# The seven products of a down projection issued between the last row tiles of the up projection, with five operands split step by step

## The chip, the core and the metric

One core of one Trainium2 chip runs the whole layer in one launch. The metric is device time in microseconds (us) of one execution; lower is better. The core has a matrix engine (TensorE, PE in the rows; PEld is its weight load), VectorE (DVE), ScalarE (ACT), GpSimd (POOL), SyncE (SP), and 16 DMA engines.

## The reference, cut to what matters

One decoder layer on 512 tokens of width 1024. The change lies in its feed-forward part:

```python
up = causal_dwconv(h @ w_up, conv_w, conv_b)      # 1024 -> 2*2816, width 3
val, gate = up[..., :D_FF], up[..., D_FF:]
ffn = (silu(gate) * val) @ w_down                 # 2816 -> 1024
h = layer_norm(ALPHA * h + ffn + ple)
```

Everything is float32. A product of two float32 matrices is formed from rounded high parts and the low parts left over (`mm3`: high x high, high x low, low x high), so each operand is first split: ScalarE copies the high part, VectorE subtracts it to give the low part.

## The kernel before, in words

**Up projection** (`ffn_up`, L1188). D_FF = 2816 makes NF = 22 row tiles f of 128 features; each has a value half (b = 0) and a gate half (b = 1). A half is 24 matmuls (8 chunks of the 1024 inputs, three each) into one PSUM bank of 128 x 512, and then a convolution: one ScalarE activation (L1200) and two VectorE multiply-adds (L1201, L1202, by the helper at L292). After both halves ScalarE does Silu (L1204, recorded at L299). A weight half tile is 512 KB; `Weights` fetches it on SP's queue (L103), splits it with a ScalarE cast (L120) and a VectorE subtraction (L121), and `use(n)` splits one ahead and fetches three ahead.

**Tiles 0 to 15** are the first 2048 rows of the down projection. They go through `combine` (L1220): even and odd tiles are paired (p = 0 to 7), tokens are cut into two halves, and the pair gives the seven left operands of a seven-product scheme for 2 x 2 block matrices (A11, S3, S2, A22, S1, A12, S4). The first four are split at once (pages `sa`, L1249 to L1252); S1, A12 and S4 are kept raw and split in one go before the product that reads them (`split_left`, L1263). **Tiles 16 to 21** are split as they come (`act`, L1208 to L1212) and multiplied in the plain way at the end.

**Right operands** (`Products`, L171). The 2048 rows of `w_down` are 2 x 2 blocks of 4 parts each. `ORDER` lists the seven right operands: three are plain blocks (products 0, 5, 6), one is a fresh block that gets a second one subtracted (product 1), and three reuse an earlier raw part and add another block (products 2, 3, 4). Subtracting is done by a ScalarE multiply by -1 (L207) and an accumulating DMA issued by GpSimd (L208), 16 of them in all. Each part is then split (L219, L220). With 7 products of 4 parts there are 28 steps, numbered 0 to 27 here; `use(n)` splits up to step n + 1 and fetches up to step n + 5.

**Down projection** (`ffn_down`, L1276). A step is 12 matmuls (2 sub-parts, 2 row blocks of 128 tokens, three each). The products accumulate in PSUM pairs X, Y and V; four of them are added to the residual in between (`add`, L1306). Then come tiles 16 to 21 with six plain weight tiles (`WD`), 162 matmuls, and the layer norm and stores (L1344 to L1361).

**What sets the order.** `run` (L1364) goes through `ffn_up` to its end and then calls `ffn_down`. The order in which each engine meets its instructions is set at build time by a planner that follows the program's order as a priority, its own model of durations, and the dependencies; each engine's queue then runs strictly in that order on the chip. Only where `self.in_order` is true (L263) are all matmuls tied to the program's order; it is false from L1390 on.

**Buffers.** `Pages` (L44) hands out 51 SBUF buffers of 128 x 1024 float32, first freed first reused. A buffer that is handed out again may be written only when the readers of its earlier content are done. So a short list of free buffers means that a fetch or a split waits for recent work. PSUM has 8 banks, handed out in the same way (`Banks`, L73).

**Fetching for the down projection** begins in the last two row tiles (L1213 to L1215): after tile 20 step 0 is split and step 1 fetched, after tile 21 step 1 is split and step 2 fetched. The layer norm's two vectors are loaded after product 2 (L1322, L1323).

Of the kernel before, what the change touches and what calls it, by code (L numbers as in the profile page):

```python
# [12 lines left out]
F32 = mybir.dt.float32  # L13
F32R = mybir.dt.float32r
I32 = mybir.dt.int32
AF = mybir.ActivationFunctionType
ALU = mybir.AluOpType

P = 128
T = 512  # L20
# [5 lines left out]
NF = DFF // P  # L26
# [3 lines left out]
NPAGES, NHALVES = 37, 6  # L30
NPAGES_LATE = 14
NS = 8
LAG_B, LAG_C = 5, 7
QK_RATIO, G_RATIO = 6.5 / 6, 7 / 6
SPLIT_AHEAD = 1
# [135 lines left out]
class Products:  # L171
# [14 lines left out]
    def __init__(self, tc, pages, blocks, fetch_ahead=5, split_ahead=1):  # L186
        self.nc, self.pages, self.blocks = tc.nc, pages, blocks
        self.fa, self.sa = fetch_ahead, split_ahead
        self.per = NS // 2
        self.raw, self.hl = {}, {}  # L190
# [45 lines left out]
class Layer:  # L236
    def __init__(self, tc, cst, pages, banks, a):
# [18 lines left out]
        self.W = Weights(tc, pages, srcs)  # L256
        self.WD = Weights(tc, pages, [a["w_down"][i] for i in range(NF - 2 * NS)], halved=False)
        self.WP = Products(tc, pages, a["w_down_blocks"])
# [927 lines left out]


    def ffn_up(self):  # L1188
        nc = self.nc
        self.act, self.left, self.now = [], {}, ([], [])  # L1190
        for f in range(NF):
            yp = self.pages.get(f"cv{f}", F32, (P, 2, T))
            for b in range(2):
                bank = self.banks.get(f"up{f}{b}")
                for _ in self.feature_mms(self.wup + 2 * f + b, bank, self.hT):
                    pass
                y = yp.t[:, b]
                cw = self.cw[:, b * NF + f]
                cb = self.cb[:, b * NF + f:b * NF + f + 1]
                nc.scalar.activation(y, bank.t, AF.Identity, scale=cw[:, 2:3], bias=cb)  # L1200
                self.stt(y[:, 1:], bank.t[:, 0:T - 1], cw[:, 1:2], y[:, 1:], ALU.mult, ALU.add)  # L1201
                self.stt(y[:, 2:], bank.t[:, 0:T - 2], cw[:, 0:1], y[:, 2:], ALU.mult, ALU.add)  # L1202
                bank.free()
            self.actf(3, yp.t[:, 1], yp.t[:, 1], AF.Silu)  # L1204
            if f < 2 * NS:
                self.combine(f, yp)
            else:
                self.tt(yp.t[:, 0], yp.t[:, 0], yp.t[:, 1], ALU.mult)  # L1208
                pg = self.pages.get(f"act{f}", F32R, (P, 2, T))
                self.split(pg.t[:, 0], pg.t[:, 1], yp.t[:, 0])  # L1210
                yp.free()
                self.act.append(pg)  # L1212
            if f >= NF - 2:  # L1213
                self.WP.split_to(f - NF + 3)
                self.WP.fetch_to(f - NF + 4)  # L1215
            yield
        for pg in self.hT:
            pg.free()

    def combine(self, f, yp):  # L1220

        nc, p = self.nc, f // 2
        first, last = slice(0, T // 2), slice(T // 2, T)
        y0, y1 = yp.t[:, 0], yp.t[:, 1]
        if f % 2 == 0:

            self.sq = self.pages.get(f"sq{p}", F32, (P, 4, T // 2))
            self.tt(self.sq.t[:, 0], y0[:, first], y1[:, first], ALU.mult)  # L1230
            self.tt(y0[:, last], y0[:, last], y1[:, last], ALU.mult)
            self.even = yp
            return
        sq, q = self.sq.t, p % 4
        if q == 0:
            for name in ("S1", "A12", "S4"):
                self.left.setdefault(name, []).append(self.pages.get(f"{name}{p}", F32, (P, 4, T // 2)))
        s1, a12, s4 = (self.left[name][-1].t[:, q] for name in ("S1", "A12", "S4"))
        a21 = self.even.t[:, 0, last]
        self.tt(a12, y0[:, first], y1[:, first], ALU.mult)  # L1240
        self.tt(sq[:, 3], y0[:, last], y1[:, last], ALU.mult)
        yp.free()
        self.tt(sq[:, 1], a21, sq[:, 0], ALU.subtract)
        self.tt(s1, a21, sq[:, 3], ALU.add)
        self.even.free()
        self.tt(sq[:, 2], s1, sq[:, 0], ALU.subtract)
        self.tt(s4, a12, sq[:, 2], ALU.subtract)
        for i in range(2):
            pg = self.pages.get(f"sa{p}{i}", F32R, (P, 2, 2, T // 2))  # L1249
            src = sq[:, 2 * i:2 * i + 2]  # L1250
            nc.scalar.copy(pg.t[:, :, 0], src)
            self.tt(pg.t[:, :, 1], src, pg.t[:, :, 0].bitcast(F32), ALU.subtract)  # L1252
            self.now[i].append(pg)
        self.sq.free()

    def load_conv(self):
        self.cw = self.cst.tile([P, 2 * NF, 3], F32, name="cw")
# [2 lines left out]
        self.nc.sync.dma_start(self.cb, self.a["conv_b"])  # L1260


    def split_left(self, name):  # L1263

        out = []
        for raw in self.left.pop(name):
            for i in range(2):
                pg = self.pages.get(f"sl{name}{i}", F32R, (P, 2, 2, T // 2))
                src = raw.t[:, 2 * i:2 * i + 2]
                self.nc.scalar.copy(pg.t[:, :, 0], src)  # L1270
                self.tt(pg.t[:, :, 1], src, pg.t[:, :, 0].bitcast(F32), ALU.subtract)
                out.append(pg)
            raw.free()
        return out

    def ffn_down(self):  # L1276


        nc, WP, WD, res = self.nc, self.WP, self.WD, [pg.t for pg in self.res]
        halves = (slice(0, 512), slice(512, 1024))  # L1280
        X, Y, V, Z = [], [], [], []
        ops = {}

        def now(i, o):
            return [[pg.t[:, o, x] for x in range(2)] for pg in self.now[i]]

        def left(name):
            ops[name] = self.split_left(name)
            return [[pg.t[:, o, x] for x in range(2)] for pg in ops[name] for o in range(2)]

        def product(q, bank, a, fresh, side=lambda j: None):
            if fresh:
                bank.extend(self.banks.get(f"p{q}{m}") for m in range(2))
            for j in range(WP.per):
                n = q * WP.per + j
                hi, lo = (pg.t.rearrange("p (k n) -> p k n", k=2) for pg in WP.use(n))
                for k in range(2):
                    p = 2 * j + k
                    for m in range(2):
                        ts_ = slice(m * P, m * P + P)  # L1300
                        self.mm3(bank[m].t, a[p][0][:, ts_], a[p][1][:, ts_], hi[:, k], lo[:, k],
                                 fresh and p == 0, p == NS - 1)
                WP.free(n)
                side(j)

        def add(bank, rows, col):  # L1306
            for m in range(2):
                r = res[2 * rows + m][:, halves[col]]
                self.tt(r, r, bank[m].t, ALU.add)

        def drop(pages):
            for pg in pages:
                pg.free()

        product(0, X, now(0, 0), True)
        add(X, 0, 0)
        product(1, Y, now(0, 1), True)
        drop(self.now[0])
        add(Y, 1, 1)
        product(2, X, now(1, 0), False)  # L1320
        add(X, 1, 0)
        g2 = self.bcast_load("ln2_g", "g2", nc.sync)  # L1322
        b2 = self.bcast_load("ln2_b", "b2", nc.sync)  # L1323
        a = left("S1")
        product(3, Y, now(1, 1), False)
        drop(self.now[1])
        product(4, X, a, False)
        drop(ops["S1"])
        add(X, 1, 1)
        product(5, V, left("A12"), True)  # L1330
        drop(ops["A12"])
        product(6, X, left("S4"), False, lambda j: WD.use(j))
        drop(ops["S4"])
        Z.extend(self.banks.get(f"z{m}") for m in range(2))
        KD = NF - 2 * NS
        ws = [WD.use(k) for k in range(KD)]

        q = slice(768, 1024)
# [5 lines left out]
        for t in range(4):  # L1344
            r, parts = res[t], parts_of[t]
            st, mv = self.ln_tiles(len(parts))
            ts_ = slice(t * P, t * P + P)
            for i, (c, bank, fresh) in enumerate(parts):
                for k in range(KD):
                    a, w = self.act[k].t, ws[k]  # L1350
# [13 lines left out]
    def run(self):  # L1364
# [36 lines left out]
                self.prefetch_mid()  # L1401
        for _ in self.mid():
            pass
        for _ in self.ffn_up():
            pass
        self.ffn_down()


# [43 lines left out]
def _rows(w, per):  # L1452

    k = w.shape[0] // P
    return w.reshape(k // per, per, P, w.shape[1]).transpose(0, 2, 1, 3).reshape(k // per, P, per * w.shape[1])
# [12 lines left out]
def layouts(i):  # L1468
# [18 lines left out]
        "w_up": up,  # L1487
        "w_down": _rows(i["w_down"][0][2 * NS * P:], 1),

# [35 lines left out]
```

## Time and profile before

| what | us |
|---|---|
| three runs of the kernel before | 804.79, 807.84, 809.76 |
| median | 807.84 |
| the profiled execution's own time | 807.08 |
| its span, first to last instruction | 805.3 |
| around the span (807.08 - 805.3) | 1.8 |

Times in the rows are counted from the span's start. "Busy" on PE includes modelled ends of matmuls, so the start times of matmuls are the safer reading.

### The profile page before, as it was taken

What the parts mean: (1) busy time and instruction counts of PE and PEld (TensorE: products, weight loads), DVE (VectorE), ACT (ScalarE), POOL (GpSimd) and SP (SyncE); (2) the same over time, 40 slices, a digit from 0 to 9 for tenths busy, and PEclk for the clock granted to TensorE, in tenths of its full rate; (3) what the DMA queues carried; (4) which work ended last, traced back from release to release, by engine and by line L of the source; (5) the groups of instructions that cost most, each with busy time, mean ns of one, the idle gap of its engine ahead of it and who ended that gap; (6) DMA issues with size and microseconds to landing.
All of it is one profiled execution on the core that took longest, in us unless ns stands there. A gap on an engine that the chain in (4) does not pass through costs nothing. (4 is left out here: it accounts for less than half of the span.)

```text
span 805.3 us, 9856 instructions
## 1 busy us (share of the span) xinstructions
PE 778.2 (97%) x3668; PEld 648.7 (81%) x3668; DVE 547.0 (68%) x960; ACT 366.8 (46%) x578; POOL 38.5 (5%) x81
## 2 busy tenths in 40 slices
PE   8999999999999989999999999999999998799996
PEld 7888888878888878888888888888888887578885
DVE  6866998696667958947744566666666664367656
ACT  6435667654443274514433344343434345577300
POOL 0000000000000010004300000000000002210000
PEclk9999999999999999999999999999999999899999
DMA  9913222024022584414212330224122327987202
GB/s 320 373 70 99 58 74 60 27 89 145 28 79 78 185 261 157 140 58 171 76 53 105 105 129 3 79 78 131 53 78 79 105 79 213 224 182 285 90 26 79
DMA packets 32176, 95.14 MB, mean 118 GB/s; under 512 B 4480, under 2 KB 8704, under 8 KB 31872
## 3 DMA queue, kind: packets, MB, share of 16 engines
q1 hardware_dynamic: 28240, 81.40, 29.7%
q0 software_dynamic: 3312, 12.06, 6.8%
q10 hardware_dynamic: 576, 1.05, 0.3%
q8 instruction: 29, 0.48, 0.2%
q14 instruction: 19, 0.16, 0.1%
HBM read 88.20 MB, written 3.15 MB: 113 GB/s over the span
## 5 line engine op out<-in xcount | busy, mean ns | idle before, releaser
L262 PE MATMUL up<-hT,wh 128*128 128x512 f32 x704 | 216.5, 389 | 0.0
L121 DVE TENSOR_TENSOR wl<-wr,wh 128x1024 fp32r<-128x1024 f32 (+1 forms) x113 | 135.7, 1212 | 59.5 <-ACT wh L120 43.2
L120 ACT CAST wh<-wr 128x1024 fp32r<-128x1024 f32 (+1 forms) x113 | 116.8, 1043 | 90.6 <-PE o L262 13.4
L262 PEld LDWEIGHTS up<-hT,wh 128*128 128x128 f32 x704 | 132.2, 188 | 27.3
L262 PE MATMUL up<-hT,wl 128*128 128x512 f32 x352 | 136.9, 389 | 0.0
L292 DVE SCALAR_TENSOR_TENSOR cv<-up,cw,cv 128x511 f32<-128x511 f32 x88 | 65.8, 748 | 35.6 <-ACT cv L1200 34.2
L262 PE MATMUL g<-xs,wh 128*128 128x512 f32 x256 | 81.0, 398 | 0.0
L262 PEld LDWEIGHTS up<-hT,wl 128*128 128x128 f32 x352 | 66.1, 188 | 13.7
L1200 ACT ACTIVATE cv<-up,cb,cw 128x512 f32<-128x512 f32 x44 | 34.3, 779 | 64.7 <-PE up L262 64.7
L262 PEld LDWEIGHTS g<-xs,wh 128*128 128x128 f32 x256 | 46.1, 188 | 8.6 <-issue 0.6
L220 DVE TENSOR_TENSOR dl<-dr,dh 128x1024 fp32r<-128x1024 f32 x28 | 33.7, 1222 | 24.5 <-ACT dh L219 24.5
L262 PE MATMUL g<-xs,wl 128*128 128x512 f32 x128 | 50.0, 391 | 0.0
L262 PE MATMUL p<-dh,sa 128*128 128x512 f32 x128 | 41.2, 400 | 7.3 <-ACT dh L219 7.3
L262 PE MATMUL mx<-yts,wh 128*128 128x512 f32 x128 | 39.2, 390 | 2.4 <-DVE yts L970 2.4
L262 PE MATMUL pg<-wh,hT 128*128 128x512 f32 x128 | 40.2, 390 | 0.0
L262 PE MATMUL o<-wh,mx 128*128 128x512 f32 x128 | 40.0, 391 | 0.0
L219 ACT CAST dh<-dr 128x1024 fp32r<-128x1024 f32 x28 | 28.5, 1046 | 15.6 <-DMA dr<-in_w_down_blocks_dram 15.6
L262 PEld LDWEIGHTS p<-dh,sa 128*128 128x128 f32 x128 | 24.6, 193 | 13.1 <-ACT dh L219 8.2
L262 PEld LDWEIGHTS mx<-yts,wh 128*128 128x128 f32 x128 | 23.9, 188 | 7.7 <-DVE yts L970 2.8
L208 POOL DMA_DIRECT2D dr<-in_w_down_blocks_dram x16 | 13.9, 869 | 311.4 <-ACT dr L207 311.1
L262 PEld LDWEIGHTS g<-xs,wl 128*128 128x128 f32 x128 | 24.0, 188 | 5.3
L262 PEld LDWEIGHTS pg<-wh,hT 128*128 128x128 f32 x128 | 24.0, 188 | 4.9
(213 smaller groups left out, 1390.1 us busy)
## 6 DMA issues: line engine op xcount, KB each, us to landing
wr<-in_w_up_dram SPq DMA_DIRECT2D x44, 512.0 KB, 3.3
wr<-in_w_g_dram SPq DMA_DIRECT2D x16, 512.0 KB, 3.4
dr<-in_w_down_blocks_dram SPq DMA_DIRECT2D x16, 512.0 KB, 5.2
dr<-in_w_down_blocks_dram POOLq DMA_DIRECT2D x16, 512.0 KB, 7.9
wr<-in_w_qk_dram SPq DMA_DIRECT2D x8, 512.0 KB, 9.9
wr<-in_w_glu_dram SPq DMA_DIRECT2D x8, 512.0 KB, 4.1
wr<-in_w_o_dram SPq DMA_DIRECT2D x8, 512.0 KB, 3.3
wr<-in_w_pe_gate_dram SPq DMA_DIRECT2D x8, 512.0 KB, 3.5
```

The source lines that it names most:

```text
L120: self.nc.scalar.copy(hi.t[:, c], raw.t[:, c])
L121: self.nc.vector.tensor_tensor(out=lo.t[:, c], in0=raw.t[:, c], in1=hi.t[:, c].bitcast(F32), op=ALU.subtract)
L208: self.nc.gpsimd.dma_start(pg.t, self.block(plus, j), accum_op=ALU.add)
L219: self.nc.scalar.copy(hi.t, raw.t)
L220: self.nc.vector.tensor_tensor(out=lo.t, in0=raw.t, in1=hi.t.bitcast(F32), op=ALU.subtract)
L262: ins = self.nc.tensor.matmul(out=out, lhsT=lhsT, rhs=rhs, start=start, stop=stop, skip_group_check=True).ins
L292: self.nc.vector.scalar_tensor_tensor(out=out, in0=a, scalar=s, in1=b, op0=op0, op1=op1)
L1200: nc.scalar.activation(y, bank.t, AF.Identity, scale=cw[:, 2:3], bias=cb)
```

## The change

`ffn_up` now yields twice per tile, after the value half and at the end. `run` fetches the right operands of steps 0 to 3 at tile 14, splits step 0 at tile 15, and from the value half of tile 16 on takes 1.5 steps of a generator `products()` per half tile: 18 of the 28 steps lie between halves of tiles 16 to 21, the other 10 behind them. From the first step on `in_order` is true. `combine` splits only A11 and S3 (two pairs at a time, buffer `se`); S2, A22, S1, A12 and S4 stay raw, and `products()` splits each in pieces of 128 x 512, one piece for this step and one for the next. The layer norm's vectors are loaded after step 19, and the tiles of `WD` are used from step 24, as before.

```diff
+PRODUCTS_RATIO = 1.5
...
     def ffn_up(self):
...
                 bank.free()
+                if b == 0:
+                    yield f
...
-            if f >= NF - 2:
-                self.WP.split_to(f - NF + 3)
-                self.WP.fetch_to(f - NF + 4)
-            yield
+            yield f
...
     def combine(self, f, yp):
+        if f % 4 == 0:
+            self.early = self.pages.get(f"se{p}", F32, (P, 2, 2, T // 2))
+        a11, s3 = (self.early.t[:, o, p % 2] for o in range(2))
...
-            for name in ("S1", "A12", "S4"):
+            for name in ("S2", "A22", "S1", "A12", "S4"):
...
-        for i in range(2):
-            pg = self.pages.get(f"sa{p}{i}", F32R, (P, 2, 2, T // 2))
-            src = sq[:, 2 * i:2 * i + 2]
-            nc.scalar.copy(pg.t[:, :, 0], src)
-            self.tt(pg.t[:, :, 1], src, pg.t[:, :, 0].bitcast(F32), ALU.subtract)
+        if p % 2 == 1:
+            for o, name in enumerate(("A11", "S3")):
+                self.ops.setdefault(name, []).append(self.split_pairs(name + str(p), self.early.t[:, o]))
+            self.early.free()
+
+    def split_pairs(self, name, src):
+        pg = self.pages.get(f"sl{name}", F32R, (P, 2, 2, T // 2))
+        self.nc.scalar.copy(pg.t[:, :, 0], src)
+        self.tt(pg.t[:, :, 1], src, pg.t[:, :, 0].bitcast(F32), ALU.subtract)
+        return pg
...
+    def products(self):
...
+        def operand(n):
+            if n >= len(todo) or todo[n] in split:
+                return
+            q, j = todo[n]
+            name = self.PRODUCTS[q][0]
+            if q < 2:
+                split[q, j] = ops[name][j]
+                return
+            raw = ops[name][j // 2]
+            split[q, j] = self.split_pairs(f"{name}{j}", raw.t[:, 2 * (j % 2):2 * (j % 2) + 2])
+            if j % 2 == 1:
+                raw.free()
+
+        for n, (q, j) in enumerate(todo):
...
+            hi, lo = (pg.t.rearrange("p (k n) -> p k n", k=2) for pg in WP.use(n))
+            operand(n)
+            operand(n + 1)
+            a = split.pop((q, j))
+            for k in range(2):
+                for m in range(2):
+                    ts_ = slice(m * P, m * P + P)
+                    self.mm3(self.acc[b][m].t, a.t[:, k, 0, ts_], a.t[:, k, 1, ts_], hi[:, k], lo[:, k],
+                             whole[b] == q and (j, k) == (0, 0), (j, k) == (WP.per - 1, 1))
+            a.free()
+            WP.free(n)
+            if j == WP.per - 1 and q in self.WHOLE:
...
+                    self.tt(r, r, self.acc[b][m].t, ALU.add)
+            yield q, j
...
     def run(self):
-        for _ in self.ffn_up():
-            pass
+        products, acc = None, 0.0
+        for f in self.ffn_up():
+            if f == 2 * NS - 2:
+                self.WP.fetch_to(self.WP.nf + 2)
+            if f == 2 * NS - 1:
+                self.WP.split_to(1)
+            if f >= 2 * NS:
+                if products is None:
+                    products = self.products()
+                    self.in_order, self.last_mm = True, None
+                acc += PRODUCTS_RATIO
+                while acc >= 1.0:
+                    acc -= 1.0
+                    next(products)
+        for q, j in products:
+            if (q, j) == (4, 3):
+                self.g2 = self.bcast_load("ln2_g", "g2", self.nc.sync)
+                self.b2 = self.bcast_load("ln2_b", "b2", self.nc.sync)
+            if q == 6:
+                self.WD.use(j)
         self.ffn_down()
```

## Rows read from the trace of the kernel before

**Rows 1.** The page: busy us and share of the span, by engine
```profile
PE 778.2 (97%) x3668; PEld 648.7 (81%) x3668; DVE 547.0 (68%) x960; ACT 366.8 (46%) x578; POOL 38.5 (5%) x81
```
**Rows 2.** Windows: PE, PEld, DVE, ACT, POOL busy (instructions), clock, DMA share, GB/s
```profile
680.00:690.00 10.00, 2.85 (x12) 2.12 (x11) 3.92 (x6) 7.11 (x10) 4.29 (x5) 0.81 1.06 237
690.00:700.00 10.00, 9.77 (x38) 7.42 (x37) 3.69 (x4) 6.27 (x7) 2.07 (x3) 0.85 1.06 210
...
611.40:676.70 65.30, 65.30 (x290) 54.09 (x289) 39.85 (x51) 29.49 (x37) 1.25 (x2) 1.00 0.33 103
...
731.70:764.60 32.90, 32.90 (x146) 27.22 (x146) 23.39 (x25) 19.28 (x22) 0.00 (x0) 1.00 0.44 160
```
**Rows 3.** Timeline of PE: start, us, instruction [idle before, its releaser]
```profile
676.75 0.39 PE L262 MATMUL p<-dh,sa 128*128 128x512 f32 x1
...
681.97 0.39 PE L262 MATMUL p<-dh,sa 128*128 128x512 f32 x1
689.50 1.22 PE L262 MATMUL p<-dh,sa 128*128 128x512 f32 x2 [7.15 <-ACT dh L219]
...
721.19 0.50 PE L262 MATMUL p<-dl,sa 128*128 128x512 f32 x1 [0.49 <-DVE dl L220]
...
759.63 0.61 PE L262 MATMUL p<-dh,slS 128*128 128x512 f32 x2
...
764.39 0.39 PE L262 MATMUL p<-dh,slS 128*128 128x512 f32 x1
764.61 0.39 PE L262 MATMUL p<-wh,act 128*128 128x512 f32 x1
```
**Rows 4.** Timeline of ACT in the hole
```profile
678.98 2.94 ACT L207 ACTIVATE dr<-dr 128x1024 f32<-128x1024 f32 x3
...
683.28 0.61 ACT L299 ACTIVATE cv<-cv 128x512 f32<-128x512 f32 x1
685.55 1.06 ACT L207 ACTIVATE dr<-dr 128x1024 f32<-128x1024 f32 x1 [1.66 <-DMA dr<-in_w_down_blocks_dram]
686.51 0.60 ACT L279 CAST act<-cv 128x512 fp32r<-128x512 f32 x1
687.46 1.99 ACT L219 CAST dh<-dr 128x1024 fp32r<-128x1024 f32 x2 [0.34 <-DMA dr<-in_w_down_blocks_dram]
```
**Rows 5.** Groups, 655 to 806 us: busy, mean ns | idle before
```profile
L220 DVE TENSOR_TENSOR dl<-dr,dh 128x1024 fp32r<-128x1024 f32 x28 | 33.7, 1222 | 24.5 <-ACT dh L219 24.5
L219 ACT CAST dh<-dr 128x1024 fp32r<-128x1024 f32 x28 | 28.5, 1046 | 15.6 <-DMA dr<-in_w_down_blocks_dram 15.6
L207 ACT ACTIVATE dr<-dr 128x1024 f32<-128x1024 f32 x16 | 16.6, 1054 | 6.1 <-DVE dl L220 3.9 <-DMA dr<-in_w_down_blocks_dram 2.1
...
L283 DVE TENSOR_TENSOR slS<-S,slS 128x512 fp32r<-128x512 f32 x8 | 5.3, 685 | 0.2 <-ACT slS L1270 0.2
...
L1270 ACT CAST slS<-S 128x512 fp32r<-128x512 f32 x8 | 4.7, 611 | 0.0
...
L1200 ACT ACTIVATE cv<-up,cb,cw 128x512 f32<-128x512 f32 x5 | 3.9, 779 | 3.6 <-PE up L262 3.6
```
**Rows 6.** DMA queues and issues, 676 to 712 us: share of 16 engines; KB, us to landing
```profile
q0 software_dynamic: 1584, 5.77, 81.2%
q1 hardware_dynamic: 831, 3.01, 22.6%
...
dr<-in_w_down_blocks_dram POOLq DMA_DIRECT2D x11, 512.0 KB, 8.6
dr<-in_w_down_blocks_dram SPq DMA_DIRECT2D x2, 512.0 KB, 6.9
```
**Rows 7.** Tile dr: duration ns min/median/max; landing min/median/max
```profile
L208 POOL DMA_DIRECT2D dr<-in_w_down_blocks_dram x16: 856/865/945, 665.5 to 720.8; - x16
...
DMA to landing us min/median/max: 3.1/6.4/11.2
```
**Rows 8.** Groups, 611.4 to 676.7 us (the last six row tiles)
```profile
L292 DVE SCALAR_TENSOR_TENSOR cv<-up,cw,cv 128x511 f32<-128x511 f32 (+1 forms) x24 | 18.0, 748 | 14.0 <-ACT cv L1200 13.6
```

More of the change, by code (lines that the diff above doesn't have):

```diff
@@ L1189, in ffn_up @@
         nc = self.nc
-        self.act, self.left, self.now = [], {}, ([], [])
+        self.act, self.ops = [], {}
         for f in range(NF):
@@ L1220, in combine @@
     def combine(self, f, yp):
-        nc, p = self.nc, f // 2
+        p = f // 2
         first, last = slice(0, T // 2), slice(T // 2, T)
         y0, y1 = yp.t[:, 0], yp.t[:, 1]
+        if f % 4 == 0:
+            self.early = self.pages.get(f"se{p}", F32, (P, 2, 2, T // 2))
+        a11, s3 = (self.early.t[:, o, p % 2] for o in range(2))
         if f % 2 == 0:
-            self.sq = self.pages.get(f"sq{p}", F32, (P, 4, T // 2))
-            self.tt(self.sq.t[:, 0], y0[:, first], y1[:, first], ALU.mult)
+            self.tt(a11, y0[:, first], y1[:, first], ALU.mult)
             self.tt(y0[:, last], y0[:, last], y1[:, last], ALU.mult)
@@ L1233, in combine @@
             return
-        sq, q = self.sq.t, p % 4
-        if q == 0:
-            for name in ("S1", "A12", "S4"):
-                self.left.setdefault(name, []).append(self.pages.get(f"{name}{p}", F32, (P, 4, T // 2)))
-        s1, a12, s4 = (self.left[name][-1].t[:, q] for name in ("S1", "A12", "S4"))
+        if p % 4 == 0:
+            for name in ("S2", "A22", "S1", "A12", "S4"):
+                self.ops.setdefault(name, []).append(self.pages.get(f"{name}{p}", F32, (P, 4, T // 2)))
+        s2, a22, s1, a12, s4 = (self.ops[name][-1].t[:, p % 4] for name in ("S2", "A22", "S1", "A12", "S4"))
         a21 = self.even.t[:, 0, last]
         self.tt(a12, y0[:, first], y1[:, first], ALU.mult)
-        self.tt(sq[:, 3], y0[:, last], y1[:, last], ALU.mult)
+        self.tt(a22, y0[:, last], y1[:, last], ALU.mult)
         yp.free()
-        self.tt(sq[:, 1], a21, sq[:, 0], ALU.subtract)
-        self.tt(s1, a21, sq[:, 3], ALU.add)
+        self.tt(s3, a21, a11, ALU.subtract)
+        self.tt(s1, a21, a22, ALU.add)
         self.even.free()
-        self.tt(sq[:, 2], s1, sq[:, 0], ALU.subtract)
-        self.tt(s4, a12, sq[:, 2], ALU.subtract)
-        for i in range(2):
-            pg = self.pages.get(f"sa{p}{i}", F32R, (P, 2, 2, T // 2))
-            src = sq[:, 2 * i:2 * i + 2]
-            nc.scalar.copy(pg.t[:, :, 0], src)
-            self.tt(pg.t[:, :, 1], src, pg.t[:, :, 0].bitcast(F32), ALU.subtract)
-            self.now[i].append(pg)
-        self.sq.free()
+        self.tt(s2, s1, a11, ALU.subtract)
+        self.tt(s4, a12, s2, ALU.subtract)
+        if p % 2 == 1:
[7 more added lines that the diff above has]
+        return pg
     def load_conv(self):
@@ L1260, in load_conv @@
         self.nc.sync.dma_start(self.cb, self.a["conv_b"])
[L1263 to L1274, printed above, removed]
+    PRODUCTS = (("A11", "X"), ("S3", "Y"), ("S2", "X"), ("A22", "Y"), ("S1", "X"), ("A12", "V"), ("S4", "X"))
@@ new lines @@
+    WHOLE = {0: (0, 0), 1: (1, 1), 2: (1, 0), 4: (1, 1)}
+    def products(self):
+        WP, ops = self.WP, self.ops
+        self.acc = {}
+        todo = [(q, j) for q in range(len(self.PRODUCTS)) for j in range(WP.per)]
+        split, whole = {}, {}
+        def operand(n):
[11 more added lines that the diff above has]
+        for n, (q, j) in enumerate(todo):
+            name, b = self.PRODUCTS[q]
+            fresh = b not in self.acc
+            if fresh:
+                self.acc[b] = [self.banks.get(f"{b}{m}") for m in range(2)]
+                whole[b] = q
+            hi, lo = (pg.t.rearrange("p (k n) -> p k n", k=2) for pg in WP.use(n))
[10 more added lines that the diff above has]
+            if j == WP.per - 1 and q in self.WHOLE:
+                rows, col = self.WHOLE[q]
+                for m in range(2):
+                    r = self.res[2 * rows + m].t[:, 512 * col:512 * col + 512]
+                    self.tt(r, r, self.acc[b][m].t, ALU.add)
+            yield q, j
@@ L1276, in ffn_down @@
     def ffn_down(self):
-        nc, WP, WD, res = self.nc, self.WP, self.WD, [pg.t for pg in self.res]
+        nc, WD, res = self.nc, self.WD, [pg.t for pg in self.res]
         halves = (slice(0, 512), slice(512, 1024))
[L1281 to L1334, printed above, removed]
+        X, Y, V = (self.acc[b] for b in "XYV")
+        g2, b2 = self.g2, self.b2
@@ L1335, in ffn_down @@
+        Z = [self.banks.get(f"z{m}") for m in range(2)]
         KD = NF - 2 * NS
```

## The prediction

> **What bounds the kernel now.** I read the page first: the matrix engine is busy for 97% of the span [rows 1], so only its idle time and its slow time can be won back. The windows by stage show where these lie [rows 2]. While the last six row tiles of the up projection run (611.4 to 676.7 us) PE has no idle time at clock 1.00, and so it is again from 731.7 to 764.6. Between them it is busy for 2.85 of 10 us, then for 9.77 of 10 but at a granted clock of 0.81 and 0.85. The timeline of PE gives the place [rows 3]: the first product matmul starts at 676.75, steps 0 and 1 run, and at 681.97 PE stops for 7.15 us until the high part of step 2 is there; short waits follow, one of 0.49 at 721.19.
>
> ScalarE's timeline says why [rows 4]. Its queue has three multiplies for the accumulating transfers (678.98, 2.94 us) ahead of the Silu of tile 21 (683.28), and a fourth (685.55, after 1.66 us of waiting for a DMA) ahead of the cast `act` (686.51). Only when these are done comes `dh` at 687.46. Counting buffers in program order, the list explains that order: at tile 21 only 2 of 51 are free, steps 2 to 5 are fetched into buffers that the last up matmuls give back, and the high part of step 2 goes into the buffer of tile 21's convolution, free only after that cast. The hole is thus a shortage of buffers and a blocked ScalarE queue, at the one moment when PE has no other work.
>
> **The size of what can be won.** Twelve half tiles take 65.30 us [rows 2], 5.44 each or 0.2267 per matmul. A step of 12 is 2.72 us, and 336 product matmuls want 336 x 0.2267 = 76.2. They took 764.61 - 676.75 = 87.86 us [rows 3]. So 11.7 us are lost: 7.15 in the one hole, the other 4.5 in short waits and low clock. The number of matmuls does not change. The floor is 807.08 - 11.7 = 795.4 us, if PE never waits.
>
> **Part by part.**
> - *Interleaving.* A tile of 48 matmuls (10.88 us) and three steps (8.16) takes 19.04 us, 6.35 per step. Right operands are fetched five steps ahead, now 31.7 us instead of 13.6. The longest path to a step is that of product 1: load 6.9, multiply 1.05, issue 0.87, accumulating transfer 8.6, cast 1.05, subtract 1.22 = 19.7 us; with 11.2 for both transfers and 0.95 for the issue it is 26.7 [rows 5 to 7]. Both are below 31.7, so the cover is 5 to 12 us. Gain 11.7; with the cover gone the bound is below zero (a rival, below).
> - *DMA work.* In the crowded stretch of 36 us, 11 accumulating transfers took 81.2% of the engines, 2.66 us each; 5.7 plain ones took 22.6%, 1.42 each [rows 6]. Steps 4 to 7 need both and two thirds of an up weight: 2.66 + 1.42 + 0.95 = 5.0 of 6.35 us. That fits; the later accumulating steps need no fresh load.
> - *Moved fetches.* Four loads at tiles 14 and 15 are 5.7 us of engine time on SP's queue, behind up weights fetched three half tiles (16 us) ahead, where I take the DMA share to be like the 0.33 of the next stretch [rows 2]: nothing. GpSimd's queue holds nothing else in this stretch. The two norm vectors move eight steps nearer to their use: from step 19 they have 8 x 2.72 + 36 x 0.2267 = 30 us against a landing of 6.9 [rows 6]. Nothing.
> - *Splits.* 28 splits of 128 x 512 (ScalarE 0.61, VectorE 0.69 [rows 5]) stay 28: 16 with `combine` and 12 in bulk become 8 and 20. Eight leave tiles 0 to 15, where PE is the bound: no gain. In the overlap VectorE has 39.85 / 6 = 6.6 us per tile [rows 2] and three times 1.22 + 0.69, so 12.4 of 19.04; ScalarE 29.49 / 6 = 4.9 and three times 1.05 + 1.05 + 0.61, so 13.0. PE hides both.
> - *The last ten steps* (27.2 us of PE) are tight on VectorE: 10 x (1.22 + 0.69) + 6 `WD` splits x 1.22 + two adds 1.4 = 27.8, and 2.9 for tile 21. That is 30.7, so 3.5 us too much if it comes with no lead. It has a third of the overlap idle to gain one, and my count gives 18 free buffers at step 17. Bounds 0 and 3.5; I take 1.0, two waits like the 0.49 of [rows 3], as 731.7 to 764.6 ran a like load (23.39 of 32.9 on VectorE [rows 2]) without a wait.
> - *The fixed order.* If an operand is late, the next up half waits behind it, though it could run. In the old order nothing was queued behind but more products. Cost nothing while the cover holds.
> - *PSUM banks.* X and Y hold four, so up has four. An eviction is 0.78 + 2 x 0.75 = 2.28 us [rows 5, 8]; a bank comes round after four half tiles with their steps, 38 us, of which filling and eviction need 7.7. About 30 us of slack: nothing. The Trainium skill's page "Perfetto Trace Analysis", section "Matmul Optimizations", speaks against this: it asks that all eight PSUM banks be used. By it each of the 12 half tiles could wait for its eviction, an estimate of 27 us more from the rows just named; the slack in the rows says no, and no row here shows up on four banks.
>
> **The sum.** 807.08 - 11.7 + 1.0 = 796.4 for an execution like the profiled one. The median of the three runs is 0.76 above that execution; I add half of it: 796.8.
>
> **The rivals.**
> - *VectorE becomes the bound at the end.* For: 30.7 against 27.2 us. Against: the lead. 795.4 + 1.0 + 3.5 = 799.9 us.
> - *The shortage of buffers moves.* The hole of 11.7 us comes back between tiles, the change does not do what it says, and the time is 807. For: my count of free buffers falls to 6 at step 0, and the fetch of step 6 goes into a buffer that step 0's matmuls free. Against: 6 is three times 2, that fetch comes five steps before use, and no step waits for the last convolution: the buffer of tile 21's goes to step 21.
> - *The accumulating transfers come late in the fixed order: slower.* Place: steps 4 to 8. It decides when the path is longer than 31.7 us; the worst rows give 26.7, and 81% plus 23% of the engines shows that they can be full [rows 6]. Price: a hole costs what it did, 11.7 with its low clock; with two, 795.4 + 23.4 = 818.8 us.
> - *Four banks are too few.* Slower too: 795.4 + 12 x 2.28 = 822.8 us. Against: 30 us of slack.
>
> **How the numbers follow.** The forecast 0.68 (its own range 794 to 798.5), VectorE at the end 0.14 (to 803), the shortage moved 0.10, late transfers 0.07, banks 0.01. One per cent of 807.84 is 8.1 us, about what a measurement of this kernel tells from no change: faster means below 799.8. That is all of the forecast and 0.06 of the VectorE case, 0.74; same takes 0.08 of it and the moved shortage, 0.18; slower 0.08. A range of 794 to 804 holds the first two cases, 0.82; its lower end is the floor less the scatter downward, since the lowest run before was 2.3 below the profiled one.
>
> **What would show it.** Right: PE idle for less than 1.5 us from 611 us to the last products, clock 1.00 in every window there, the plain matmuls of tiles 16 to 21 start near 753 instead of 764.61, ScalarE's waits for `dr` transfers far below 15.6 us [rows 5], the chain from the end on PE for longer than before. VectorE as the bound: PE waits for `dl`, `sl` or `wl` subtractions in the last 27 us, VectorE above 95% there. Shortage moved: PE waits for `dh` between tiles 16 and 18, SP issuing `dr` only as matmuls end. Late transfers: ScalarE waits for DMA ahead of `dh` at steps 4 to 8 with the DMA share above 0.9. The forecast is wrong if any single PE hole above 2 us stands in the stretch.

## The result, and the profile after

The changed kernel takes 795.78 us (median of 6 runs, 794.59 to 799.43) against 808.82 for the kernel before (6 runs, 804.79 to 812.83): a ratio of 0.9841, 95% interval 0.9805 to 0.9877. The profiled execution took 794.98 us with a span of 793.3; the prediction was 796.8.

The windows of the changed kernel, with the columns of [rows 2]:

```profile
600.00:620.00 20.00, 20.00 (x90) 16.55 (x89) 11.27 (x19) 10.21 (x14) 2.49 (x3) 1.00 0.57 137
620.00:640.00 20.00, 19.24 (x85) 15.62 (x84) 12.35 (x14) 14.87 (x17) 4.39 (x6) 1.00 1.02 260
640.00:660.00 20.00, 20.00 (x90) 16.57 (x89) 15.25 (x18) 14.61 (x17) 3.45 (x4) 1.00 0.85 179
660.00:680.00 20.00, 20.00 (x90) 16.55 (x89) 13.18 (x16) 11.10 (x14) 2.59 (x3) 1.00 0.57 124
680.00:700.00 20.00, 20.00 (x90) 16.56 (x89) 15.23 (x18) 10.26 (x13) 0.00 (x0) 1.00 0.41 121
...
730.00:740.00 10.00, 10.00 (x46) 8.29 (x45) 9.72 (x12) 5.71 (x8) 0.00 (x0) 1.00 0.54 199
740.00:752.50 12.50, 12.50 (x57) 10.36 (x56) 3.94 (x4) 2.90 (x3) 0.00 (x0) 1.00 0.00 1
```

PE is busy without a break at clock 1.00, the 2.4 GHz level, but for 0.76 us between 620 and 640. The slices of [rows 2] with 2.85 of 10 us have no counterpart. Its timeline has one wait, and the first matmul of the plain part (tile 16, bank V) answers to the last row of [rows 3]:

```profile
638.62 0.50 PE L263 MATMUL up<-hT,wl 128*128 128x512 f32 x1 [0.76 <-DVE wl L122]
...
752.54 0.39 PE L263 MATMUL V<-wh,act 128*128 128x512 f32 x1
```

That is 752.54 instead of 764.61. The up projection began 1.4 us earlier in this execution (first matmul at 435.96 against 437.39 before), which is scatter (over the fourteen traces of this case it starts between 434.18 and 440.05, kernels with and without the change mixed), so the stretch from there to the plain part went from 327.2 to 316.6 us: 10.6 us, out of 11.7 to be had. The tail behind it is as long as before (40.8 and 40.7 us).

Where the 0.76 us come from is told by the chain that ended last, in order of time:

```profile
610.43 7.43 DMA dr<-in_w_down_blocks_dram
617.89 0.04 ACT dr L208
...
618.85 1.04 ACT wh L121
619.89 0.02 issue
619.92 1.24 DVE wl L122
...
621.59 6.92 DMA dr<-in_w_down_blocks_dram
...
637.34 1.24 DVE wl L122
638.58 0.04 issue
638.62 5.29 PE up L263 x22
```

Loads for product 1 (7.43 and 6.92 us) hold ScalarE's multiply, behind which stands the cast of an up weight; that weight's low part comes 0.76 us late. This is the first third of the overlap, between steps 3 and 4, with the DMA engines full (share 1.02). The right operands themselves are in time. The loads of steps 4 and 5, then of 6 and 7, are issued at 610.01 and 621.17, and step 4, the first of product 1, begins at 643.75:

```profile
610.01 0.80 SPq L204 DMA_DIRECT2D dr<-in_w_down_blocks_dram  x2
621.17 1.22 SPq L204 DMA_DIRECT2D dr<-in_w_down_blocks_dram  x2
...
643.75 0.39 PE L263 MATMUL Y<-dh,slS 128*128 128x512 f32 x1
```

That is 33.7 us ahead for step 4, and 33.4 for step 6 (654.62). What ScalarE waits for between 600 and 755 us, in us in total, times, and longest:

```profile
ACT dr L208 <- DMA dr<-in_w_down_blocks_dram: 7.6, 4, 3.1
...
ACT dh L220 <- DMA dr<-in_w_down_blocks_dram: 2.8, 2, 2.2
```

The casts wait 2.8 us for transfers where they waited 15.6 before [rows 5]; the four multiplies of product 1 wait 7.6 us for their loads.

One thing the planner does in both kernels is not in the program's order. The first accumulating transfer of the kernel before is issued at 665.52, when only the parts of steps 0 and 1 have been fetched (655.23 and 660.40); product 4 alone adds to a part of product 0, so this transfer is for step 16, which PE begins at 731.97. In the changed kernel two such transfers go out at 595.96 and 609.69, and product 4 begins at 719.90. So the crowd of transfers holds some that nothing needs for a long time. What holding them back would give was not run.

### The profile page after: what moved, and what is told of

It reads as the page before. It is cut to its first block, busy times and chain, and to the rows that moved or that the text cites. A ratio compares the mean times of both kernels' runs of the same rounds, so it can differ in the third digit from the quotient of the medians.

```text
span 793.3 us, 9840 instructions
## 1 busy us (share of the span) xinstructions
PE 775.9 (98%) x3668; PEld 648.2 (82%) x3668; DVE 545.9 (69%) x960; ACT 366.0 (46%) x578; POOL 38.4 (5%) x81
## 3 DMA queue, kind: packets, MB, share of 16 engines
q10 hardware_dynamic: 576, 1.05, 0.4%
## 4 chain that ended last, share of the span: by engine, by line
PE 88%; DMA 4%; DVE 3%; ACT 3%; issue 1%; SPq 1%; DVEq 0%; ACTq 0%
PE up L263 28%; PE g L263 10%; PE o L263 5%; PE pg L263 5%; PE X L263 5%; PE mx L263 5%; PE z L263 4%; PE Y L263 4%; PE V L263 4%; PE u L263 3%; PE v L263 3%; PE kb L263 2%; PE qb L263 2%; DMA dr<-in_w_down_blocks_dram 2%; PE A L263 2%; DMA y<-yst 2%
## 5 line engine op out<-in xcount | busy, mean ns | idle before, releaser
L263 PE MATMUL X<-dh,slS 128*128 128x512 f32 x96 | 30.4, 389 | 0.0
L263 PEld LDWEIGHTS o<-wh,mx 128*128 128x128 f32 x128 | 24.0, 188 | 4.9
L263 PE MATMUL z<-sp,tri 128*128 128x128 f32 (+3 forms) x160 | 27.2, 300 | 0.0
```

What stands on the lines that cost most here:

```text
L263: ins = self.nc.tensor.matmul(out=out, lhsT=lhsT, rhs=rhs, start=start, stop=stop, skip_group_check=True).ins
```

## The experiments

The theory after the result was that the steps between up halves give the right operands time to arrive. Its rivals: the early fetches alone do it; the four buffers saved do it; the fixed order does it. Each ratio is to the kernel before on the same chip; the changed kernel's 0.9841 is the mark to compare with. The planner makes a new order for every kernel, so a run changes more than the lines of its edit.

**No interleaving** (`e1_after_up`), of the changed kernel:

```diff
-PRODUCTS_RATIO = 1.5
+PRODUCTS_RATIO = 0.0
```

> All of the change but the interleaving: early fetches and stepwise splits stay, the 28 steps run behind tile 21. Theory (the steps between up halves give each operand a lead of about 32 us and give the matrix engine other work meanwhile): steps 0 to 3 are ready, but from step 4 on the path of 19.7 us (load, multiply, accumulating transfer, split) meets a lead of 10.9 us, so a hole of 5 to 10 us comes back behind step 3, 801 to 807 us. Rival 1 (the early fetches alone remove the hole) and rival 2 (fewer buffers held by operands remove it): 795 to 797 us, no hole above 2 us.

Measured: 808.92 us, ratio 1.0016 (0.9999 to 1.0033). All of the gain is gone. Its PE timeline has a hole of 4.75 us, and four more waits of 0.21 to 0.92 us. The hole is not behind step 3, as expected, but at the low part of step 3 itself, a plain part whose load was issued at 576.71. The queues show why, ScalarE's and VectorE's ahead of it:

```profile
687.53 0.79 PE L263 MATMUL X<-dl,slA 128*128 128x512 f32 x1 [4.75 <-DVE dl L221]
```

```profile
680.65 1.06 ACT L208 ACTIVATE dr<-dr 128x1024 f32<-128x1024 f32 x1 [1.90 <-DMA dr<-in_w_down_blocks_dram]
...
683.46 1.06 ACT L208 ACTIVATE dr<-dr 128x1024 f32<-128x1024 f32 x1 [1.23 <-DMA dr<-in_w_down_blocks_dram]
```

```profile
682.26 0.69 DVE L284 TENSOR_TENSOR cv<-cv 128x512 f32<-128x512 f32 x1 [3.84 <-ACT cv L300]
685.05 0.69 DVE L281 TENSOR_TENSOR act<-cv,act 128x512 fp32r<-128x512 f32 x1 [2.10 <-ACT act L280]
...
686.26 3.49 DVE L221 TENSOR_TENSOR dl<-dr,dh 128x1024 fp32r<-128x1024 f32 x3
```

ScalarE's multiplies wait for loads of product 1, tile 21's convolution stands behind them, and VectorE's queue, which waits for the convolution, holds the subtraction that PE needs. An operand fetched 100 us early is late all the same. The windows from there on, first whole, then three pieces of 2 us:

```profile
676.00:690.00 14.00, 9.25 (x36) 7.26 (x36) 7.14 (x9) 10.35 (x14) 3.60 (x5) 0.86 1.05 220
690.00:700.00 10.00, 9.79 (x38) 7.41 (x37) 6.25 (x8) 8.54 (x11) 4.14 (x5) 0.85 0.96 171
700.00:710.00 10.00, 8.33 (x29) 6.23 (x28) 5.21 (x7) 5.60 (x7) 0.86 (x1) 0.83 1.05 252
```

```profile
688.00:690.00 2.00, 2.00 (x6) 1.52 (x6) 2.00 (x3) 2.00 (x4) 0.17 (x1) 0.50 1.07 213
694.00:696.00 2.00, 2.00 (x10) 1.63 (x9) 2.00 (x3) 2.00 (x5) 0.86 (x1) 1.00 1.03 199
708.00:710.00 2.00, 2.00 (x6) 1.60 (x5) 1.47 (x2) 2.00 (x4) 0.00 (x0) 0.50 1.08 236
```

The hole is shorter than before, but the clock falls twice: to about 0.50, the 1.2 GHz level, from 686 to 692 with the hole and behind it, and again from about 707 to 710 after two waits of 0.92 and 0.76 us; between them it is 1.00. The 0.83 to 0.86 of the three long windows are means of the two levels. The DMA share is 0.96 to 1.05. From 665 to 710 the engines carry 13 accumulating transfers. Early fetches, fewer buffers and stepwise splits together win nothing without the interleaving: neither rival 1 nor rival 2 makes the gain by itself.

**The early fetches alone** (`e2_early_fetch`), of the kernel before:

```diff
-            if f >= NF - 2:
-                self.WP.split_to(f - NF + 3)
-                self.WP.fetch_to(f - NF + 4)
+            if f == 2 * NS - 2:
+                self.WP.fetch_to(4)
+            if f == 2 * NS - 1:
+                self.WP.split_to(1)
```

> The kernel before with only the fetch moved: steps 0 to 3 fetched at tile 14, step 0 split at tile 15. Rival 1 (early fetches alone): 795 to 798 us, no hole. Theory: the hole changes its place, as four loads are gone from the crowd but the accumulating transfers of steps 4 to 7 still start at the end of tile 21 and 22 buffers are held: 800 to 808 us.

Measured: 815.83 us, ratio 1.0097 (1.0066 to 1.0129): slower than before, outside what the theory expected. One hole of 12.00 us stands at the high part of step 2, and GpSimd's second accumulating transfer is issued at 680.88, against 676.39 before. The queue is the same as above: the cast for step 2, whose load was issued by 593, stands behind multiplies that wait for the loads of product 1, and these loads are issued only from 679.63 on, against 671.28 before.

```profile
695.92 1.06 ACT L207 ACTIVATE dr<-dr 128x1024 f32<-128x1024 f32 x1 [2.18 <-DMA dr<-in_w_down_blocks_dram]
696.89 1.97 ACT L219 CAST dh<-dr 128x1024 fp32r<-128x1024 f32 x2
```

The four parts fetched early hold buffers that the later fetches then lack; that this is why those loads are later is my count, not a run.

**Four operands split at once** (`e3_four_split`): of the changed kernel, S2 and A22 go the way of A11 and S3.

```diff
+        if p % 2 == 0:
+            self.late = self.pages.get(f"sf{p}", F32, (P, 2, 2, T // 2))
+        s2, a22 = (self.late.t[:, o, p % 2] for o in range(2))
...
+            for o, name in enumerate(("S2", "A22")):
+                self.ops.setdefault(name, []).append(self.split_pairs(name + str(p), self.late.t[:, o]))
+            self.late.free()
...
-            if q < 2:
+            if name in ("A11", "S3", "S2", "A22"):
```

> The change with four operands split at once in the up projection (A11, S3, S2, A22), as before: 22 instead of 18 buffers held when the steps begin, 2 instead of 6 free at step 0 by my count. Rival 2 (the buffers are the cause): a hole of several us between tiles 16 and 18, 801 to 808 us. Theory (the lead is the cause): 795 to 798 us, short waits below 3 us in all.

Measured: 796.18 us, ratio 0.9852 (0.9825 to 0.9879), with one PE wait of 0.62 us at 638.52. With only 2 buffers free by my count nothing is lost that can be told: with the steps interleaved, a short list of buffers makes no hole, and splitting S2 and A22 late gives nothing by itself.

**Free order** (`e4_free_order`): of the changed kernel, `in_order` stays false.

```diff
-                    self.in_order, self.last_mm = True, None
+                    pass
```

> The change without the fixed order of the matmuls: the planner may put up halves ahead of late steps. Theory: the order written in the program is also its priority, so 794.5 to 797 us and the 0.76 us wait at most gone. Rival 3 (the fixed order is what places the steps between the halves): the steps drift behind tile 21, a hole comes back, 800 to 807 us.

Measured: 793.58 us, ratio 0.9827 (0.9794 to 0.986), no wait on PE between 611 and 765 us. The planner keeps nearly the same order; at 638.23 it puts some matmuls of Y into an up half, at the place where the changed kernel waits 0.76 us. So the fixed order neither makes the gain nor costs anything that these runs can tell from 0.9841.

What then makes the hole? Two kernels take the accumulating transfers apart, both of the kernel before.

**No accumulating** (`e5_no_accumulate`) and **no multiply** (`e9_no_multiply`):

```diff
             if plus:
-                self.nc.scalar.mul(pg.t, pg.t, -1.0)
-                self.nc.gpsimd.dma_start(pg.t, self.block(plus, j), accum_op=ALU.add)
```

with both lines gone in the first and only the multiply gone in the second.

> The kernel before without the 16 multiplies by -1 and the 16 accumulating transfers (the second block is left out of the right operands of products 1 to 4); loads, splits, buffers and order stay. If the accumulating transfers fill the DMA engines and hold up ScalarE's queue, and so make the hole: steps 0 and 1 (5.4 us) nearly cover the convolution of tile 21 (4.9 us and a split of 2.3), at most 2 us of the hole stay, 796 to 800 us. If the shortage of buffers makes it: step 2 still waits for the buffer of tile 21 and the fetches for those of the last weights, 4 us or more stay, 801 to 806 us.

> The kernel before without the 16 multiplies by -1 on ScalarE; the accumulating transfers stay (so the right operands of products 1 to 4 get a sum where a difference belongs). If the time of the transfers makes the hole: 803 to 808 us, the DMA share still above 0.95 from 680 to 710 us. If it is ScalarE's queue, stuck behind multiplies that wait for their loads: most of the hole goes, 795 to 800 us.

Measured: 794.8 us, ratio 0.985 (0.9806 to 0.9893) without transfers and multiplies, and 809.13, ratio 1.0002 (0.9977 to 1.0026), without the multiplies. The first gains as much as the change, with products still behind tile 21, the 22 buffers and the convolution's buffer as before: its only wait there is 0.46 us. In the second the hole only moves (1.74 us at 681.68, 5.00 at 694.81). The lines are from the second: its ScalarE timeline behind tile 21 and its DMA queues from 676 to 712 us:

```profile
686.31 1.05 ACT L218 CAST dh<-dr 128x1024 fp32r<-128x1024 f32 x1 [4.68 <-DMA dr<-in_w_down_blocks_dram]
691.28 1.04 ACT L218 CAST dh<-dr 128x1024 fp32r<-128x1024 f32 x1 [3.93 <-DMA dr<-in_w_down_blocks_dram]
```

```profile
q0 software_dynamic: 1719, 6.26, 88.9%
q1 hardware_dynamic: 563, 2.05, 14.8%
...
dr<-in_w_down_blocks_dram POOLq DMA_DIRECT2D x12, 512.0 KB, 10.6
```

From 681 us on ScalarE has nothing in its queue here but the casts, and they wait for the transfers; the DMA share is 1.06 from 680 to 710. So the accumulating transfers are the cause of the hole: with them and without the multiplies the loss stays, without both it goes. 88.9% of 36 us for 6.26 MB in parts of 0.524 is 2.7 us each, as in [rows 6], and PE takes 2.72 us for a step. That the full engines count, and not the longer path of a step that gets a transfer more, is an argument from the share; no run separates the two.

**The multiplies on VectorE** (`e10_vector_multiply`), of the kernel before:

```diff
-                self.nc.scalar.mul(pg.t, pg.t, -1.0)
+                self.nc.vector.tensor_scalar(out=pg.t, in0=pg.t, scalar1=-1.0, scalar2=None, op0=ALU.mult)
```

> The kernel before with the 16 multiplies moved from ScalarE to VectorE, nothing else. ScalarE's queue theory: Silu and cast of tile 21 no longer wait behind the multiplies, the 7.15 us hole shrinks to 3 us or less, 797 to 803 us; VectorE, which subtracts for the same steps, may take over the blocking, then 804 to 808. Transfer theory: 804 to 808 us, the hole stays.

Measured: 813.83 us, ratio 1.0062 (1.0038 to 1.0085), a hole of 6.28 us at 689.29 and a new one of 2.45 for a `dl` subtraction at 717.27. VectorE has taken the blocking over; the expectation allowed at most 808 us for that.

```profile
686.86 0.69 DVE L207 TENSOR_SCALAR dr<-dr 128x1024 f32<-128x1024 f32 x1 [3.25 <-DMA dr<-in_w_down_blocks_dram]
687.47 0.69 DVE L280 TENSOR_TENSOR act<-cv,act 128x512 fp32r<-128x512 f32 x1
```

Here, as in the run without interleaving and in the one with the early fetches alone, a multiply that waits for its load holds up the queue in which it stands. This run alone does not clear ScalarE's queue; the one without multiplies does.

**Fewer steps in the overlap** (`e6_half_step` and `e7_one_step`), of the changed kernel, with 0.5 and 1.0:

```diff
-PRODUCTS_RATIO = 1.5
+PRODUCTS_RATIO = 0.5
```

> The change with 0.5 steps per half tile: 6 of 28 steps in the overlap, 22 behind it. Theory (transfers need more time than the steps give them behind the up projection, so they must be spread): the accumulating transfers of steps 6 to 19 still crowd behind tile 21, 3 to 9 us of the loss stay, 798 to 805 us. Rival (only the first steps after tile 21 matter, since the end of the convolution is what they wait for): 795 to 797.5 us.

> The change with one step per half tile: 12 steps in the overlap, 16 behind it. Theory: most accumulating transfers are through by the end of tile 21, 0 to 3 us of the loss stay, 794.5 to 798.5 us. Rival: as with 1.5, 794.5 to 796.5 us, and as with 0.5.

Measured: 806.99 us, ratio 0.998 (0.9964 to 0.9997) with 6 steps, and 800.94, ratio 0.9901 (0.9874 to 0.9927) with 12. Both are worse than expected. Ordered by steps in the overlap the ratios are 1.0016 (0), 0.998 (6), 0.9901 (12) and 0.9841 (18). But the holes are not where the theory put them. PE's wait with 6 steps, and ScalarE's timeline ahead of it:

```profile
708.87 0.79 PE L263 MATMUL X<-dh,slS 128*128 128x512 f32 x1 [9.86 <-ACT slS L1258]
```

```profile
702.56 1.99 ACT L220 CAST dh<-dr 128x1024 fp32r<-128x1024 f32 x2 [1.51 <-DMA dr<-in_w_down_blocks_dram]
707.25 1.04 ACT L220 CAST dh<-dr 128x1024 fp32r<-128x1024 f32 x1 [2.70 <-DMA dr<-in_w_down_blocks_dram]
708.20 0.61 ACT L1258 CAST slS<-S 128x512 fp32r<-128x512 f32 x1
```

The last GpSimd issue came at 698.85; six plain loads are issued between 693.51 and 712 and meet the accumulating transfers, and the planner has put casts that wait for transfers ahead of the left operand that PE needs. With 12 steps it is VectorE, which is busy 10.00 of 10 us from 700 to 710:

```profile
717.89 0.68 DVE L281 TENSOR_TENSOR act<-cv,act 128x512 fp32r<-128x512 f32 x1
718.49 0.69 DVE L284 TENSOR_TENSOR slA<-A,slA 128x512 fp32r<-128x512 f32 x1
719.09 2.35 DVE L221 TENSOR_TENSOR dl<-dr,dh 128x1024 fp32r<-128x1024 f32 x2
```

```profile
721.50 0.80 PE L263 MATMUL X<-dl,slS 128*128 128x512 f32 x1 [4.05 <-DVE dl L221]
```

So behind tile 21 it is first the transfers and then the splits that PE seems to outrun, and both would want the steps spread. This is read from one trace of each kernel; no run takes the splits away.

**Three steps ahead** (`e8_ahead3`), of the changed kernel:

```diff
-    def __init__(self, tc, pages, blocks, fetch_ahead=5, split_ahead=1):
+    def __init__(self, tc, pages, blocks, fetch_ahead=3, split_ahead=1):
```

> The change with right operands fetched three steps ahead instead of five: the lead falls from 31.7 to 19.0 us, and the path of product 1 is 19.7 us with the median transfers and 26.7 with the longest. Theory with the lead as I took it: steps 4 to 7 wait in turn, 2 to 10 us, 797 to 806 us. Rival (the planner issues a fetch as soon as a buffer is free, so the lead is set by the buffers and not by this number): 794.5 to 797 us.

Measured: 798.06 us, ratio 0.9869 (0.9835 to 0.9903), which cannot be told from 0.9841. No PE wait stands at steps 4 to 7; the two that there are (0.85 and 1.55 us, at 734.40 and 736.68) are for splits of A12, step 20 on. The number does move the fetches: the loads of product 1 are issued at 616.40, 619.34, 627.50 and 635.66, against 610.01 and 621.17 (two each) with five, so about 27 us ahead of their steps (step 4 begins at 643.63, step 6 at 654.51) and not 33. It is still not the 19.0 us of the count, and 27 us are just enough for the 26.7 us that the prediction took for the longest path. So the rival does not hold either: both the number and what the planner does with it set the lead.

**One bank for up** (`e11_one_bank`) and **late fetches** (`e12_late_fetch`), of the changed kernel; the first withholds three banks from step 0 to the end of the overlap, the second leaves out the fetches at tile 14 and the split at tile 15:

```diff
+                    held = [self.banks.get(f"hold{i}") for i in range(3)]
...
+        for pg in held:
+            pg.free()
```

```diff
-            if f == 2 * NS - 2:
-                self.WP.fetch_to(self.WP.nf + 2)
-            if f == 2 * NS - 1:
-                self.WP.split_to(1)
```

> The change with three more PSUM banks withheld while the steps run between up halves: one bank for the 12 half tiles instead of four. My count of slack, taken to its end: with one bank the next half waits for its eviction (2.28 us) behind steps of 2.72 or 5.44 us, so 0 to 0.5 us per half while ScalarE is prompt and 2 to 5 us at the few places where its queue waits: 797 to 808 us. If banks are as dear as the rule on eight banks says, each of the 12 halves pays at least its eviction: 822 us or more.

> The change without the fetches at tile 14 and the split at tile 15: steps 0 to 5 are fetched when step 0 is issued. The first steps meet their loads: a wait of 0 to 9 us at step 0 (load 6.9, cast and subtraction 2.3), less what the planner takes forward, and the transfers of product 1 come one tile later: 796 to 806 us. If the early fetches cost or give nothing: 795 to 796.5 us.

Measured: 802.45 us, ratio 0.9909 (0.9881 to 0.9936) with one bank; 801.79, ratio 0.9911 (0.988 to 0.9941) with late fetches. PE's waits, first with one bank, then with late fetches:

```profile
644.39 0.79 PE L263 MATMUL up<-hT,wl 128*128 128x512 f32 x1 [4.25 <-DVE wl L122]
...
685.43 0.70 PE L263 MATMUL up<-hT,wh 128*128 128x512 f32 x2 [0.18 <-DVE cv L293]
...
705.10 0.71 PE L263 MATMUL up<-hT,wh 128*128 128x512 f32 x2 [0.38 <-DVE cv L293]
...
725.93 0.70 PE L263 MATMUL up<-hT,wh 128*128 128x512 f32 x2 [1.53 <-DVE cv L293]
```

```profile
644.10 0.79 PE L263 MATMUL up<-hT,wl 128*128 128x512 f32 x1 [5.17 <-DVE wl L122]
```

The profiled execution with one bank is its slowest of ten (806.56; the others took 798.0 to 804.06), so the waits of the median run may be shorter. Evictions cost 0.18 + 0.38 + 1.53 = 2.1 us in it even on a single bank. The larger wait in both is at the place where the changed kernel waits 0.76: an up weight's low part at about 640 us, behind the transfers of product 1. How the withheld banks lengthen that wait stays open.

## Why the prediction was right

The time lay 1.0 us below the forecast and inside its own range. The sum asks only how much PE time is lost between 676.75 and 764.61 and whether spreading the steps gives it back; it does not use the cause of the loss. So it came out right though the cause was misread. The signs named for it came too: 0.76 us of idle time, clock 1.00 throughout, 752.54 where 753 was forecast, 2.8 us of cast waits where there had been 15.6. Step by step:

- **The size.** 11.7 us to be had, 10.6 measured in the stretch, 0.76 us of waiting left; the rest of the 12.1 us between the two profiled executions is the 1.4 us ahead of the up projection.
- **The residue** of 1.0 us was right in size by luck, since its place and its engine were wrong. I put it on VectorE in the last ten steps; there VectorE runs at 9.72 of 10 us and PE does not wait. It came between steps 3 and 4, on a weight of the up projection. The lead of 31.7 us and its cover held: 33.7 and 33.4 us measured, and no product matmul waited. What was missed lies in the "Splits" step, where ScalarE's 13.0 us per tile of 19.04 were called hidden: this mean leaves out that its multiplies wait for loads (7.6 us), with casts of up weights behind them. The "DMA work" step has the same fault. Its mean of 5.0 in 6.35 us hid that the planner bunches the transfers and brings those of product 4 forward: the share is 1.02 from 620 to 640 and 0.41 from 680 to 700.
- **The cause of the hole**, "a shortage of buffers and a blocked ScalarE queue", names the last link and not what sets the loss. (The queue held more than [rows 4] shows: a further multiply at 682.32 stands ahead of the Silu, so there were five, not four.) Without the multiplies the loss is as large (1.0002), with fewer buffers held and early fetches it stays (1.0016), and without the transfers it goes with as many buffers held (0.985). I had the number: an accumulating transfer takes 2.66 us of all engines, a step of product 1 needs one and a plain load, 4.08 us, and behind tile 21 PE takes a step in 2.72. I set the 4.08 only against the new pace of 6.35, not against the old. Over the four steps of product 1 that is 5.4 us too much. Over steps 0 to 15, by the same rows, it is 8 x 1.42 + 12 x 2.66 = 43.3 us against 43.5 of PE: an estimate that leaves no room for transfers brought forward or for a late start. The rest of the 11.7 us is not worked out.
- **Moved fetches at nothing.** They cost nothing, but left out they lose about 0.7% (0.9911), and alone they make the old order slower by 1% (1.0097). In these runs they pay only together with the interleaving.
- **Splits.** Splitting S2 and A22 step by step gives nothing by itself (0.9852). The rival "VectorE becomes the bound" lost here, but shows with 12 steps in the overlap, where PE waits 4.05 us for a subtraction.
- **The Trainium skill's rule on eight banks** ("Perfetto Trace Analysis", "Matmul Optimizations") did not bite with four, and with one bank the evictions cost 2.1 us, not the 27 of a wait at every half. The slack held, as far as evictions go.
- **The fixed order** costs nothing that shows (0.9827 without it). That version has the lowest median and no PE wait at all in the stretch, but it cannot be told from the changed kernel.

## What to carry to other kernels

Where a hole follows a change of stage, compare each resource's time per step with the matrix engine's time per step in that stage: here 4.08 us of transfers met 2.72 us of matmuls in the steps of product 1, and neither the early fetches, nor fewer buffers held, nor a shorter queue, as they were tried, won anything. Spreading the steps over a stage where the transfer engines were two thirds idle did, and the first fetches ahead of it gave the last 0.7%. The engine named in a wait is the last link: take the suspected link away by itself before the cause is believed. And an operand fetched early is no help while its split stands in a queue behind an instruction that waits for a later load.

## What the runs showed of the hardware that was not expected

An accumulating transfer costs about 1.8 times a plain one of the same 512 KB on the 16 DMA engines: 2.7 us (88.9% of 36 us for 6.26 MB without the multiplies) against 1.5 (39.2% of 36 us for 5.02 MB, in the same stretch of the kernel without accumulating). And a hole's price goes on after it: in the run without interleaving PE stood for 4.75 us until 687.53 and was then busy without a break from 688 to 692, but at a granted clock of 0.50, its 1.2 GHz level, and it was back at 1.00 only from 694 on. The kernel before does the same after its 7.15 us (0.50 from 688 to 692).
